# Log-sum-exp over rows of 1024: where the closing barrier waits for the last store, and which engine checks the last sums' upper range

## The chip, the cores and the metric

One core of one Trainium2 chip. The metric is the device time of one execution in microseconds (us); a kernel is quoted by the median of its runs.

## The reference

```
x: float32 [32, 512, 1024]                  # 16384 rows of 1024
max_x = max(x, axis=-1)
out   = max_x + log(sum(exp(x - max_x)))    # float32 [32, 512]
```

## The kernel before

The 67 MB of input are loaded once, in 16 loads of shrinking size, into a ring on chip. ScalarE takes exponentials without subtracting the maximum; VectorE, or ScalarE's own accumulator for a few rows, adds them up; ScalarE takes the logarithm. Dropping the maximum is safe only if each sum lies in a range, so the kernel checks the sums at the end. Every bad sum adds at least 1e17 to `count` by a matmul, and `count` below 1e15 means "all fine". If not, a branch leads to a slow, safe program. The data never take it.

```python
def check(c0, c1, i):                       # called for sums 0..118, and last for 119..126
    first = nc.vector.tensor_scalar(out=clamped[:, c0:c1], in0=sumexp[:, c0:c1],
        scalar1=LOW, scalar2=HIGH, op0=ALU.max, op1=ALU.min)
    counted = nc.vector.scalar_tensor_tensor(out=clamped[:, c0:c1], in0=clamped[:, c0:c1],
        scalar=0.0, in1=sumexp[:, c0:c1], op0=ALU.bypass, op1=ALU.not_equal,
        accum_out=bad[:, i : i + 1])
    nc.tensor.matmul(count, lhsT=bad[:, i : i + 1], rhs=far, start=i == 0, stop=False)
# ... loads, exponentials, sums (cut) ...
nc.scalar.activation(out=res[:, W:NC], in_=sumexp[:, W:NC], func=AF.Ln)          # L208
nc.sync.dma_start(out=out_rows, in_=res[:, 0:W])                                 # L209
last_store = nc.sync.dma_start(out=out_rest, in_=res[:, W:NC]).ins               # L210
# ... check of the last row, check(LATE, LAST, 1), two more matmuls into count (cut) ...
nc.vector.tensor_scalar(out=fine, in0=count, scalar1=HIGH, scalar2=None, op0=ALU.is_lt)
all_fine = nc.values_load(fine[0:1, 0:1], engines=ENGINES, ...)                  # ScalarE, VectorE
with tc.If(all_fine < 1, ...):                                                   # the safe program (cut)
```

The program closes with a barrier that the framework writes. Each engine reports by a drain that adds 1 to a "gather" semaphore; GpSimdE's **collecting** instruction waits for 4 reports, its **releasing** instruction lets the others go on, then GpSimdE **clears** the kernel's semaphores, and a second barrier of the same kind ends the program. In front of its report, SyncE waits for everything that is open. The kernel before arranges that the store is the last item of that list:

```python
def look_at_store_last(program):
    # ... find SyncE's drain with the long list of waits (cut) ...
    waits = sorted(drain.sync_info.on_wait, key=lambda wait: wait.id != store)
```

Of the kernel before, what the change touches and what calls it, by code (L numbers as in the profile page):

```python
# [9 lines left out]
LOW, HIGH = 1e-15, 1e15  # L10
# [4 lines left out]
def kernel(  # L15
# [5 lines left out]
    nc = tc.nc  # L21
# [5 lines left out]
    ALU = mybir.AluOpType  # L27
# [4 lines left out]
    NC = n // P  # L32
# [29 lines left out]
    LATE = 119  # L62
    LAST = NC - 1
# [6 lines left out]
    sumexp = stats.tile([P, NC], fp32, name="sumexp")  # L70
    res = stats.tile([P, NC], fp32, name="res")
    clamped = stats.tile([P, NC], fp32, name="clamped")
    bad = stats.tile([P, 4], fp32, name="bad")
    fine = stats.tile([1, 1], i32, name="fine")
    far = stats.tile([P, 1], fp32, name="far")
    ones = stats.tile([P, 1], fp32, name="ones")
    last_exp = psum.tile([P, d], fp32, name="last_exp")
    count = psum.tile([1, 1], fp32, name="count")
# [5 lines left out]
    def source(e0, size):  # L84

        assert e0 >= W * d or e0 + size <= W * d
        return x_rest[:, e0 - W * d : e0 - W * d + size] if e0 >= W * d else x_rows[:, e0 : e0 + size]

    def without_wait(ins, group, reason):

        tc.declare_no_dep(ins.ins, group=group, reason=reason)

    def in_this_order(first, then):

        info = mybir.DependencyInfo(mybir.DependencyClass.NoSync, mybir.DependencyReason.DATA)
        tc.add_manual_dep(then.ins, first.ins.name, info, reason="order on one engine")


    def check(c0, c1, i):
        first = nc.vector.tensor_scalar(  # L100
            out=clamped[:, c0:c1], in0=sumexp[:, c0:c1],
            scalar1=LOW, scalar2=HIGH, op0=ALU.max, op1=ALU.min,
        )
        counted = nc.vector.scalar_tensor_tensor(  # L104
            out=clamped[:, c0:c1], in0=clamped[:, c0:c1], scalar=0.0, in1=sumexp[:, c0:c1],
            op0=ALU.bypass, op1=ALU.not_equal, accum_out=bad[:, i : i + 1],
        )
        nc.tensor.matmul(count, lhsT=bad[:, i : i + 1], rhs=far, start=i == 0, stop=False)  # L108
        return first, counted

    ln = counted = None
    c = 0
# [3 lines left out]
    for i, (size, ops) in enumerate(loads):  # L116
        if here + size > RING * d:
            assert here == p
            p = here = 0
        dma = nc.sync.dma_start(out=ring[:, here : here + size], in_=source(done, size)).ins  # L120
        if i == 0:
            first_load = dma
        end = here + size
        done += size
        for k, (how, s) in enumerate(ops):
            rows = ring[:, p : p + s * d].rearrange("p (c d) -> p c d", d=d)
            sums = sumexp[:, c : c + s]
            if how == "A":
                assert here == p
                v = ring[:, p : p + d]  # L130
                o = v if c < LAST else last_exp
                exp = nc.scalar.activation(out=o, in_=v, func=AF.Exp, accum_out=sums)  # L132
                here += d
            else:
                upto = end if k + 1 == len(ops) else p + s * d
                v = ring[:, here:upto]
                exp = nc.scalar.activation(out=v, in_=v, func=AF.Exp)  # L137
                here = upto
            assert p + s * d <= here <= end
            without_wait(exp, "loads", "the slot's earlier users came before this load")  # L140
            without_wait(exp, "exps", "the slot's earlier users came before this load")
            without_wait(exp, "sums", "the slot's earlier users came before this load")
            tc.add_to_no_dep_group("exps", exp.ins)
            if ln:
                in_this_order(ln, exp)
                ln = None
            added = []
            if how == "R":
                added = [nc.vector.reduce_sum(out=sums, in_=rows, axis=AX.X)]  # L149
            elif how == "T":  # L150
                for r in range(s):
                    lo = rows[:, r, 0:H]
                    added.append(
                        nc.vector.scalar_tensor_tensor(  # L154
                            out=lo, in0=lo, scalar=1.0, in1=rows[:, r, H:d],
                            op0=ALU.mult, op1=ALU.add, accum_out=sums[:, r : r + 1],
                        )
                    )
            for add in added:
                tc.declare_no_dep(add.ins, dma, reason="ScalarE has waited for it")  # L160
                without_wait(add, "loads", "they came before this one")
            for add in added:
                tc.add_to_no_dep_group("sums", add.ins)
                if counted:
                    in_this_order(counted, add)
                    counted = None
            c += s
            p += s * d
            last_row = v
        assert here == end  # L170
        tc.add_to_no_dep_group("loads", dma)
        if c == LATE:
            ln = nc.scalar.activation(out=res[:, 0:W], in_=sumexp[:, 0:W], func=AF.Ln)  # L173
            in_this_order(exp, ln)
            _, counted = check(0, LATE, 0)

    def start_early(program):

# [9 lines left out]
        )  # L188
        top.insert(k, first)

    def look_at_store_last(program):


        block, k, drain = next(
            (b, k, i) for b in program.main_func.blocks for k, i in enumerate(b.instructions)
            if i.engine == mybir.EngineType.SP and isinstance(i, mybir.InstDrain)
            and i.sync_info and len(i.sync_info.on_wait) > 2
        )
        store = last_store.sync_info.on_update[0].id
        waits = sorted(drain.sync_info.on_wait, key=lambda wait: wait.id != store)  # L200
        assert waits[0].id == store and len(waits) == len(drain.sync_info.on_wait)
        sync = mybir.SyncInfo(on_wait=waits, on_update=list(drain.sync_info.on_update))
        block.instructions[k] = drain.__replace__(sync_info=sync)

    nc.at_finalize(start_early)
    nc.at_finalize(look_at_store_last)

    nc.scalar.activation(out=res[:, W:NC], in_=sumexp[:, W:NC], func=AF.Ln)  # L208
    nc.sync.dma_start(out=out_rows, in_=res[:, 0:W])  # L209
# [5 lines left out]
    low = nc.vector.tensor_scalar(  # L215
        out=bad[:, 2:3], in0=bad[:, 3:4], scalar1=LOG_LOW, scalar2=None, op0=ALU.is_lt
    )
    first, _ = check(LATE, LAST, 1)
    in_this_order(add, seen)
    in_this_order(low, first)  # L220
    nc.tensor.matmul(count, lhsT=bad[:, 2:3], rhs=far, start=False, stop=False)  # L221
    nc.tensor.matmul(count, lhsT=sumexp[:, LAST:NC], rhs=ones, start=False, stop=True)  # L222
    nc.vector.tensor_scalar(out=fine, in0=count, scalar1=HIGH, scalar2=None, op0=ALU.is_lt)  # L223
    all_fine = nc.values_load(
        fine[0:1, 0:1], engines=ENGINES, min_val=0, max_val=1,
# [2 lines left out]
    with tc.If(all_fine < 1, preferred_fallthrough_block=False):  # L228
        with tc.tile_critical(sync_engine=mybir.EngineType.Activation):
            with nc.semaphore("landed") as landed, nc.semaphore("ready") as ready:  # L230
                rows = 0
                steps = 0
                for c0 in range(0, NC, RING):
# [6 lines left out]
                    for c1, c2 in ((c0, edge), (edge, c0 + s)):  # L240
                        if c1 == c2:
                            continue
                        nc.scalar.dma_start(
                            out=ring[:, (c1 - c0) * d : (c2 - c0) * d],
# [5 lines left out]
                        out=neg, in_=v, op=ALU.max, axis=AX.X, negate=True  # L250
# [3 lines left out]
                        out=v, in0=v, in1=neg[:, :, None].to_broadcast([P, s, d])  # L254
# [5 lines left out]
                        out=sumexp[:, c0 : c0 + s], in_=v, axis=AX.X  # L260
# [40 lines left out]
```

## Time and profile before

| | before |
|---|---|
| time | 163.34 us, median of 3 runs (163.11 to 163.40) |
| span in the profile | 161.6 us |
| DMA engines occupied | 97.1% of the span |
| busy: VectorE, ScalarE, TensorE | 115.0, 117.0, 0.5 us |
| from ScalarE's last update (the last sum) to the end of the span | 2.455 us |

Two things help in reading it. The views count only engine work, so the last 1.9 us of the span look empty; there one reads the instructions of the line on which the framework's closing code is booked (L296 here, another number in each kernel). And the trace records each semaphore update with its time. No view prints these, so where I use them I give the number in plain text. The prediction below shows the lines of the page, the chain and the timeline.

### The profile page before, as it was taken

The page shows a single profiled execution, that of the slowest core. Times are in us where ns is not written, and L with a number is a line of the kernel's source. Part 1 is how long each engine was busy: PE and PEld are TensorE (multiplying, and loading weights), DVE is VectorE, ACT ScalarE, POOL GpSimd, SP SyncE. Part 2 cuts the span into 40 slices and gives each one's busy share as a digit, 9 for nine tenths or more (in the row PEclk, how much of TensorE's full clock was granted, in tenths as well). Part 3 has the DMA queues.
Part 4 walks back from the last instruction along what each step waited for, and adds up shares of the span by engine and source line. Part 5 has one row for each costly group of instructions (what it writes and reads, how often), then busy time and mean ns, then how long its engine had stood idle before and what let it go on. Part 6 is the DMA issues. An engine that isn't in the chain of part 4 may idle for free.

```text
span 161.6 us, 227 instructions
## 1 busy us (share of the span) xinstructions
PE 0.5 (0%) x8; PEld 0.3 (0%) x8; DVE 115.0 (71%) x62; ACT 117.0 (72%) x59; POOL 0.2 (0%) x4
## 2 busy tenths in 40 slices
PE   0000000000000000000000000000000000000000
PEld 0000000000000000000000000000000000000000
DVE  0000000899929999399999999999499947995683
ACT  3000059990799609994299949974999999999994
POOL 0000000000000000000000000000000000000000
DMA  8995996996996997998899999996999899999990
GB/s 260 519 519 260 519 519 276 503 519 276 503 519 292 487 519 308 470 519 357 381 438 438 438 422 406 494 520 292 438 438 479 373 456 408 426 430 421 407 378 7
DMA packets 2594, 67.19 MB, mean 416 GB/s; under 512 B 544, under 2 KB 544, under 8 KB 928
## 3 DMA queue, kind: packets, MB, share of 16 engines
q1 hardware_dynamic: 2592, 67.18, 97.1%
q14 instruction: 2, 0.02, 0.0%
HBM read 67.11 MB, written 0.07 MB: 416 GB/s over the span
## 4 chain that ended last, share of the span: by engine, by line
DMA 59%; ACT 19%; DVE 17%; another core or an unknown queue 3%; issue 1%; SPq 0%; PE 0%
DMA ring<-in_x_dram 59%; ACT ring L137 19%; DVE sumexp L149 15%; DVE ring L154 1%; SPq L120 0%; DVE bad L214 0%; PE count L108 0%; DVE clamped L104 0%; DVE bad L215 0%; DVE fine L223 0%; DVE clamped L100 0%; PE count L222 0%; PE count L221 0%
## 5 line engine op out<-in xcount | busy, mean ns | idle before, releaser
L149 DVE TENSOR_REDUCE sumexp<-ring 128x8 f32<-128x8192 f32 (+6 forms) x17 | 102.9, 6107 | 39.7 <-ACT ring L137 39.7
L137 ACT ACTIVATE ring<-ring 128x8192 f32<-128x8192 f32 (+14 forms) x24 | 98.9, 4175 | 41.5 <-DMA ring<-in_x_dram 41.5
L132 ACT ACTIVATE ring<-ring 128x1024 f32<-128x1024 f32 x15 | 15.6, 1043 | 0.0
L154 DVE SCALAR_TENSOR_TENSOR ring<-ring 128x512 f32<-128x512 f32 x17 | 10.9, 687 | 3.5 <-ACT ring L137 3.5
L132 ACT ACTIVATION_READ_ACCUMULATOR ring<-ring 128x1 f32 x15 | 2.8, 189 | 0.0
L80 ACT ACT_TABLE_LOAD x1 | 1.3, 1283 | 0.8 <-PEq L285 0.8
L154 DVE DVE_READ_ACCUMULATOR ring<-ring 128x1 f32 x17 | 1.4, 83 | 0.0
L132 ACT ACTIVATE last_exp<-ring 128x1024 f32<-128x1024 f32 x1 | 1.0, 1013 | 0.0
L108 PE MATMUL count<-far,bad 128*1 128x1 f32 x4 | 0.4, 164 | 159.1 <-DVE clamped L104 159.1
L81 DVE MEMSET ones<- 128x1 f32 x1 | 0.1, 59 | 0.9 <-PEq L285 0.9
L104 DVE SCALAR_TENSOR_TENSOR clamped<-clamped,sumexp 128x119 f32<-128x119 f32 (+1 forms) x2 | 0.5, 226 | 0.1
L108 PEld LDWEIGHTS count<-far,bad 128*1 128x1 f32 x4 | 0.2, 80 | 159.2 <-DVE clamped L104 159.2
L223 DVE TENSOR_SCALAR fine<-count 1x1 int32<-1x1 f32 x1 | 0.1, 145 | 0.4 <-PE count L222 0.4
L100 DVE TENSOR_SCALAR clamped<-sumexp 128x119 f32<-128x119 f32 (+1 forms) x2 | 0.4, 190 | 0.0
L214 DVE TENSOR_REDUCE bad<-ring 128x1 f32<-128x64 f32 x1 | 0.2, 220 | 0.1
L173 ACT ACTIVATE res<-sumexp 128x112 f32<-128x112 f32 x1 | 0.3, 282 | 0.0
L208 ACT ACTIVATE res<-sumexp 128x16 f32<-128x16 f32 x1 | 0.2, 216 | 0.0
L222 PE MATMUL count<-ones,sumexp 128*1 128x1 f32 x2 | 0.2, 164 | 0.0
L221 PE MATMUL count<-far,bad 128*1 128x1 f32 x2 | 0.2, 163 | 0.0
L132 ACT ACTIVATION_READ_ACCUMULATOR last_exp<-ring 128x1 f32 x1 | 0.2, 187 | 0.0
L215 DVE TENSOR_SCALAR bad<-bad 128x1 f32<-128x1 f32 x1 | 0.2, 154 | 0.0
L104 DVE DVE_READ_ACCUMULATOR clamped<-clamped,sumexp 128x1 f32 x2 | 0.2, 83 | 0.0
(7 smaller groups left out, 0.7 us busy)
## 6 DMA issues: line engine op xcount, KB each, us to landing
ring<-in_x_dram SPq DMA_DIRECT2D x1, 6912.0 KB, 31.7
ring<-in_x_dram SPq DMA_DIRECT2D x1, 6400.0 KB, 26.4
ring<-in_x_dram SPq DMA_DIRECT2D x1, 4608.0 KB, 25.1
ring<-in_x_dram SPq DMA_DIRECT2D x1, 3840.0 KB, 23.4
ring<-in_x_dram SPq DMA_DIRECT2D x1, 2816.0 KB, 25.8
ring<-in_x_dram SPq DMA_DIRECT2D x1, 2048.0 KB, 30.1
ring<-in_x_dram SPq DMA_DIRECT2D x1, 1792.0 KB, 22.5
ring<-in_x_dram SPq DMA_DIRECT2D x1, 1408.0 KB, 25.5
```

The source lines that it names most:

```text
L80: nc.scalar.preload_act_table_set("natural_log_exp_and_others")
L100: first = nc.vector.tensor_scalar(out=clamped[:, c0:c1], in0=sumexp[:, c0:c1], scalar1=LOW, scalar2=HIGH, op0=ALU.max, op1=ALU.min,)
L104: counted = nc.vector.scalar_tensor_tensor(out=clamped[:, c0:c1], in0=clamped[:, c0:c1], scalar=0.0, in1=sumexp[:, c0:c1], op0=ALU.bypass, ...
L108: nc.tensor.matmul(count, lhsT=bad[:, i : i + 1], rhs=far, start=i == 0, stop=False)
L132: exp = nc.scalar.activation(out=o, in_=v, func=AF.Exp, accum_out=sums)
L137: exp = nc.scalar.activation(out=v, in_=v, func=AF.Exp)
L149: added = [nc.vector.reduce_sum(out=sums, in_=rows, axis=AX.X)]
L154: nc.vector.scalar_tensor_tensor(out=lo, in0=lo, scalar=1.0, in1=rows[:, r, H:d], op0=ALU.mult, op1=ALU.add, accum_out=sums[:, r : r + 1],)
L173: ln = nc.scalar.activation(out=res[:, 0:W], in_=sumexp[:, 0:W], func=AF.Ln)
L208: nc.scalar.activation(out=res[:, W:NC], in_=sumexp[:, W:NC], func=AF.Ln)
L214: seen = nc.vector.reduce_max(out=bad[:, 3:4], in_=last_row[:, 0 : d // 16], axis=AX.X)
L215: low = nc.vector.tensor_scalar(out=bad[:, 2:3], in0=bad[:, 3:4], scalar1=LOG_LOW, scalar2=None, op0=ALU.is_lt)
```

## The change

Two parts, both at the very end. **Part 1** takes the wait for the last store out of SyncE's list and puts it on GpSimdE's collecting instruction, which saves the steps from SyncE to the barrier. **Part 2** takes the upper limit out of the late check: TensorE adds the late sums themselves into `count`, so a sum above 1e15 pushes `count` over the limit by itself. One small VectorE operation goes, eight matmuls of one column come. The operands of the last sum's matmul change places too (last line of the diff).

```diff
+    def check_late():
+        for c in range(LATE, LAST):
+            nc.tensor.matmul(count, lhsT=ones, rhs=sumexp[:, c : c + 1], start=False, stop=False)
+        low = nc.vector.scalar_tensor_tensor(
+            out=clamped[:, LATE:LAST], in0=sumexp[:, LATE:LAST], scalar=LOW,
+            in1=sumexp[:, LATE:LAST], op0=ALU.max, op1=ALU.not_equal, accum_out=bad[:, 1:2],
+        )
+        nc.tensor.matmul(count, lhsT=bad[:, 1:2], rhs=far, start=False, stop=False)
 ... (check_early is the old check for sums 0 to 118; cut)
-    def look_at_store_last(program):
+    def wait_for_store_in_barrier(program):
 ... (the same search for SyncE's drain; the store's wait is taken out of its list; cut)
+        k, collect = next(
+            (k, i) for k, i in enumerate(block.instructions)
+            if i.engine == mybir.EngineType.Pool and isinstance(i, mybir.InstEventSemaphore)
+        )
+        sync = mybir.SyncInfo(
+            on_wait=moved + list(collect.sync_info.on_wait),
+            on_update=list(collect.sync_info.on_update),
+        )
+        block.instructions[k] = collect.__replace__(sync_info=sync)
 ...
-    nc.tensor.matmul(count, lhsT=sumexp[:, LAST:NC], rhs=ones, start=False, stop=True)
+    nc.tensor.matmul(count, lhsT=ones, rhs=sumexp[:, LAST:NC], start=False, stop=True)
```

More of the change, by code (lines that the diff above doesn't have):

```diff
@@ L96, in in_this_order, with check_early @@
         tc.add_manual_dep(then.ins, first.ins.name, info, reason="order on one engine")
-    def check(c0, c1, i):
-        first = nc.vector.tensor_scalar(
-            out=clamped[:, c0:c1], in0=sumexp[:, c0:c1],
+    def check_early():
+        nc.vector.tensor_scalar(
+            out=clamped[:, 0:LATE], in0=sumexp[:, 0:LATE],
             scalar1=LOW, scalar2=HIGH, op0=ALU.max, op1=ALU.min,
@@ L104, in check @@
         counted = nc.vector.scalar_tensor_tensor(
-            out=clamped[:, c0:c1], in0=clamped[:, c0:c1], scalar=0.0, in1=sumexp[:, c0:c1],
-            op0=ALU.bypass, op1=ALU.not_equal, accum_out=bad[:, i : i + 1],
-        )
-        nc.tensor.matmul(count, lhsT=bad[:, i : i + 1], rhs=far, start=i == 0, stop=False)
-        return first, counted
+            out=clamped[:, 0:LATE], in0=clamped[:, 0:LATE], scalar=0.0, in1=sumexp[:, 0:LATE],
+            op0=ALU.bypass, op1=ALU.not_equal, accum_out=bad[:, 0:1],
+        )
+        nc.tensor.matmul(count, lhsT=bad[:, 0:1], rhs=far, start=True, stop=False)
+        return counted
+    def check_late():
[6 more added lines that the diff above has]
+        nc.tensor.matmul(count, lhsT=bad[:, 1:2], rhs=far, start=False, stop=False)
+        return low
     ln = counted = None
@@ L174 @@
             in_this_order(exp, ln)
-            _, counted = check(0, LATE, 0)
+            counted = check_early()
     def start_early(program):
@@ L199, in look_at_store_last @@
         store = last_store.sync_info.on_update[0].id
-        waits = sorted(drain.sync_info.on_wait, key=lambda wait: wait.id != store)
-        assert waits[0].id == store and len(waits) == len(drain.sync_info.on_wait)
-        sync = mybir.SyncInfo(on_wait=waits, on_update=list(drain.sync_info.on_update))
-        block.instructions[k] = drain.__replace__(sync_info=sync)
+        waits = list(drain.sync_info.on_wait)
+        moved = [wait for wait in waits if wait.id == store]
+        assert len(moved) == 1
+        sync = mybir.SyncInfo(
+            on_wait=[wait for wait in waits if wait.id != store],
+            on_update=list(drain.sync_info.on_update),
+        )
+        block.instructions[k] = drain.__replace__(sync_info=sync)
+        k, collect = next(
+            (k, i) for k, i in enumerate(block.instructions)
+            if i.engine == mybir.EngineType.Pool and isinstance(i, mybir.InstEventSemaphore)
+        )
+        sync = mybir.SyncInfo(
+            on_wait=moved + list(collect.sync_info.on_wait),
+            on_update=list(collect.sync_info.on_update),
+        )
+        block.instructions[k] = collect.__replace__(sync_info=sync)
     nc.at_finalize(start_early)
-    nc.at_finalize(look_at_store_last)
+    nc.at_finalize(wait_for_store_in_barrier)
     nc.scalar.activation(out=res[:, W:NC], in_=sumexp[:, W:NC], func=AF.Ln)
@@ L217 @@
     )
-    first, _ = check(LATE, LAST, 1)
+    first = check_late()
     in_this_order(add, seen)
```

## The prediction

> **What bounds the kernel now.** I read the page first, then the chain that ended last in order of time, then the timeline of the last 3 us, then the groups of the closing line 296 and the waits of the DMA queue, and last the trace's own records of semaphore updates, which no view prints (times from the span's start; I name each one I use).
>
> The page, for the size of things:
>
> ```profile
> span 161.6 us, 227 instructions
> PE 0.5 (0%) x8; PEld 0.3 (0%) x8; DVE 115.0 (71%) x62; ACT 117.0 (72%) x59; POOL 0.2 (0%) x4
> q1 hardware_dynamic: 2592, 67.18, 97.1%
> DMA 59%; ACT 19%; DVE 17%; another core or an unknown queue 3%; issue 1%; SPq 0%; PE 0%
> ```
>
> The DMA engines are occupied for 97.1% of the span. The input, 67.11 MB, sets about 153.5 us of the 161.6. Nothing in the change touches a load, a ring slot, an exponential or a large sum. TensorE and GpSimdE are practically idle. So all that can move is what follows the last loads:
>
> ```profile
> 125.70 27.82 DMA ring<-in_x_dram
> 153.52 0.02 issue
> 153.55 3.51 ACT ring L137 x2
> ...
> 158.81 0.16 DVE L100 TENSOR_SCALAR clamped<-sumexp 128x8 f32<-128x8 f32 x1
> 158.94 0.19 ACT L132 ACTIVATION_READ_ACCUMULATOR last_exp<-ring 128x1 f32 x1
> 159.01 0.17 DVE L104 SCALAR_TENSOR_TENSOR clamped<-clamped,sumexp 128x8 f32<-128x8 f32 x1
> 159.16 0.22 ACT L208 ACTIVATE res<-sumexp 128x16 f32<-128x16 f32 x1
> 159.32 0.11 PEld L222 LDWEIGHTS count<-ones,sumexp 128*1 128x1 f32 x2
> 159.40 0.34 SPq L210 DMA_DIRECT2D out_dram<-res  x1
> 159.57 0.14 DVE L223 TENSOR_SCALAR fine<-count 1x1 int32<-1x1 f32 x1 [0.38 <-PE count L222]
> ```
>
> (The first three lines are of the chain, the others of the timeline.) Two paths leave the last exponential. The **store path**: logarithm L208, store L210 issued at 159.40. The **branch path**: range check on VectorE, sums on TensorE, comparison L223 at 159.57, then the load of the flag into registers and the branch. The printed chain goes down the branch path, but it ends at the last engine work, 159.71, and the span is 161.6: the missing 1.9 us lie in instructions it does not count:
>
> ```profile
> out_dram<-res SPq DMA_DIRECT2D x1, 8.0 KB, 1.4
> SPq L296 <- DVEq L228: 0.6, 1, 0.6
> L296 SPq EVENT_SEMAPHORE  x8: 17/28/624, 159.8 to 161.5; - x8
> L296 POOLq EVENT_SEMAPHORE  x4: 17/17/17, 160.9 to 161.5; - x4
> L296 SPq DRAIN  x3: 7/7/7, 160.8 to 161.1; - x3
> ```
>
> The store lands 1.4 us after its issue. SyncE walks through its list of waits (the 624 ns one is its wait for VectorE's branch), and GpSimdE's collecting instruction runs at 160.9. In exact records: the last of the store's 16 increments comes at 160.817; SyncE's drain, which waits for it, starts at 160.834; its next drain, which reports to the barrier, at 160.889; the report is in at 160.897; GpSimdE collects at 160.921 and its update shows at 160.946; the span ends at 161.589. VectorE's report had come at 160.805, ScalarE's at 160.680, TensorE's at 159.589. So **the store binds the end**, then two SyncE drains, then the barrier. The branch path is 12 ns short of it by VectorE's report.
>
> **What the Trainium skill says.**
> - "DMA: Bandwidth & Descriptors", section "Anatomy of one DMA", puts most of a DMA's fixed cost of about 2 us on the write receipt, after which the semaphore moves. That is for the GpSimdE path; here 8 KB from SyncE take 1.42 us from issue to last increment. The change leaves it as it is.
> - "Perfetto Trace Analysis", section "Sequencer-only Instruction (DRAIN, etc)": the profiler starts such an instruction when all its semaphores are satisfied, and neither the wait nor the propagation of its update is in its duration. The trace agrees in what matters: a drain of 7 ns costs 55 ns from start to the next one's (160.834 to 160.889), so the duration is no measure of a hop. For an event instruction with two waits it differs, since the 624 ns one contains its second wait.
> - "VectorE: DVE Perf Modes", section "The DRAIN you can't avoid", says that a semaphore after each operation costs nothing extra. The trace agrees: the 128x512 sums of L154 start 613 ns apart where each updates a semaphore (151.255, 151.868) and 612 ns where none does (153.968, 154.580).
>
> **Part 1: the wait for the store moves to GpSimdE.** Removed from the path: SyncE's start after the increment (17 ns), the step to its second drain (55), its report (8) and GpSimdE's start after it (24): 160.817 to 160.921, 104 ns. Put there: GpSimdE's own start after the last increment, taken as the same 24 ns as after a report. An event instruction with two waits lasts 28 ns on SyncE against 17 with one, so 11 ns more. Sum: 104 - 24 - 11 = **69 ns saved**, provided that all four reports are in by 160.82. SyncE's is: in the built program it has one wait instruction less (five and a drain, against six and a drain), and its steps are 61 ns. VectorE's, at 160.805, is just in time even without part 2.
>
> **Part 2: the upper check by TensorE.** One small VectorE operation goes (L100 on 128x8). The remaining one can start where that one did, 158.814; its result followed its start by 186 ns (159.009 to 159.195), so it comes at 159.000. TensorE must now wait for the last sum instead, whose ScalarE update is at 159.134. It starts 42 ns after an update (159.195 to 159.237), so at 159.176, and from the first weight load of L222 to the last update it takes 227 ns (159.317 to 159.544): 159.403, against 159.544. The branch path gains **141 ns**: VectorE reports at about 160.66, SyncE at about 160.61. None of it is on the path that sets the end, which is the store's. It buys distance to it, 12 ns becoming about 150.
> Added are eight matmuls of one column for the late sums. Each runs as two passes, about 26 ns apart in the trace, so 8 x 52 = 0.42 us of TensorE. Each waits for its own sum only; the last of these is ready by 158.4 (VectorE 158.40, ScalarE 158.09), 0.7 us before TensorE is needed. They are hidden. VectorE's seven added updates cost nothing, as above. The early half of the check is unchanged.
>
> **Sum:** 69 ns from part 1, 0 from part 2. 163.34 - 0.07 = **163.27 us**.
>
> **Rivals.**
> 1. The branch path takes the store's place. For it: it is only 12 ns behind in this one execution, and the order of the two may change from one execution to another. Against: part 2 takes 141 ns from it. Where the store had landed sooner before, the gain comes from the branch path and is about as large (up to 0.15 us): 163.2.
> 2. The added matmuls are done one after another at the end, if TensorE's order or its waits hold them back. Then up to 0.42 us come on to the branch path, less 0.14 that it gains and 0.15 of distance: 163.4 to 163.5. Against: the listing of the built program has each matmul waiting on one sum's own count.
> 3. GpSimdE reacts to a DMA's semaphore more slowly than SyncE does. No record shows GpSimdE waiting for a DMA. If it took 100 ns in place of 24, the gain would be nothing: 163.34.
> 4. The whole is drowned in what executions differ by. The three runs before lie 0.29 us apart, four times the gain. This is nearly sure for the timed runs: the sign of the measured difference is little better than a coin's, perhaps 65 to 35 for faster.
>
> **Range and chances.** The median of three runs, each spread by about 0.15 us around its middle, with a shift of 0 to -0.15, gives 163.0 to 163.55 for 8 in 10. 2% is 3.3 us; nothing here is of that size, whichever rival holds: faster 0.01, same 0.98, slower 0.01.
>
> **What would show each step right or wrong.** In the trace of the changed kernel: GpSimdE's first closing event instruction should start, or end, within 25 to 45 ns of the store's last increment, and the span should end 0.70 us after that increment instead of 0.772. SyncE should report some 0.2 us before the store lands, VectorE some 0.15. The timeline should show the eight added matmuls spread over 153 to 158.5 us and L223's successor about 0.14 us earlier relative to the end of the last accumulator read. If that comparison is later, rival 2 holds; if GpSimdE starts over 80 ns after the increment, rival 3; if a report comes after the store, rival 1. The predicted time would be wrong if the loads themselves moved, by a change of over 0.3 us in the time of the last load's landing (153.5), for which I see no cause.

## The result

The changed kernel took 163.29 us (163.23 to 163.30, 6 runs) against 163.33 us before (163.11 to 163.48, 6 runs). The ratio is 0.9998, with a 95% interval of 0.9985 to 1.0011: the same.

The page of the changed kernel, the lines that answer to those of before:

```profile
span 161.5 us, 257 instructions
PE 1.9 (1%) x24; PEld 1.0 (1%) x24; DVE 114.9 (71%) x61; ACT 117.0 (72%) x59; POOL 0.2 (0%) x4
q1 hardware_dynamic: 2592, 67.18, 97.1%
```

TensorE has 16 more matmul records (eight matmuls of two passes), VectorE one operation less, and the loads are as they were. The timeline of the changed kernel's last microseconds (start, length, engine, line, operation):

```profile
158.40 0.24 PE L114 MATMUL count<-sumexp,ones 128*1 128x1 f32 x4 [0.42 <-DVE ring L165]
...
158.76 0.16 DVE L115 SCALAR_TENSOR_TENSOR clamped<-sumexp 128x8 f32<-128x8 f32 x1
158.84 0.08 DVE L115 DVE_READ_ACCUMULATOR clamped<-sumexp 128x1 f32 x1
158.89 0.19 ACT L143 ACTIVATION_READ_ACCUMULATOR last_exp<-ring 128x1 f32 x1
...
159.13 0.09 PEld L246 LDWEIGHTS count<-sumexp,ones 128*1 128x1 f32 x2
...
159.35 0.34 SPq L234 DMA_DIRECT2D out_dram<-res  x1
159.36 0.15 DVE L247 TENSOR_SCALAR fine<-count 1x1 int32<-1x1 f32 x1 [0.44 <-PE count L246]
```

Before, the comparison came 0.17 us after the store's issue (159.57 and 159.40); now the two come together. In the list of instructions that touch `count`, the added matmuls stand with their count, their durations in ns (minimum, median, maximum) and their first and last start:

```profile
L114 PE MATMUL count<-sumexp,ones x16: 163/164/165, 154.1 to 158.5; 128*1 128x1 f32 x16
```

They end before TensorE is needed for the last checks at 158.97. The closing code of the changed kernel, in the same form:

```profile
L320 SPq EVENT_SEMAPHORE  x7: 17/28/448, 159.7 to 161.4; - x7
L320 POOLq EVENT_SEMAPHORE  x4: 17/17/43, 160.8 to 161.4; - x4
...
L320 SPq DRAIN  x3: 7/7/7, 160.5 to 161.0; - x3
...
L320 POOLq EVENT_SEMAPHORE_RANGE_CLEAR  x1: 113/113/113, 161.1 to 161.1; - x1
```

SyncE's longest wait, the one for the branch, fell from 624 to 448 ns. SyncE is at its drains at 160.5, where before it stood at 160.8 because of the store. One GpSimdE instruction now lasts 43 ns, where all lasted 17: it is the collecting one, with two waits.

By the trace's own records the store's last increment is at 160.765. GpSimdE's collecting instruction starts 24 ns later (104 before), its update comes 75 ns after the increment (129 before), and the span ends 0.719 us after it (0.772 before). So **the closing path is 53 ns shorter**. The span is 105 ns shorter, but the other 52 ns are not the change's. The store's increment itself came 52 ns sooner, of which 44 ns were there already at the start of the exponential of 128x2304 behind the last large load (153.547 before, 153.503 after).

### The profile page after: what moved, and what is told of

Same layout as the page of the kernel before. It is cut to its first block, busy times and chain, and to the rows that moved or that the text cites. A ratio compares the mean times of both kernels' runs of the same rounds, so it can differ in the third digit from the quotient of the medians. Undisturbed runs are those within 1.5% of the kernel's fastest.

```text
span 161.5 us, 257 instructions
## 1 busy us (share of the span) xinstructions
PE 1.9 (1%) x24; PEld 1.0 (1%) x24; DVE 114.9 (71%) x61; ACT 117.0 (72%) x59; POOL 0.2 (0%) x4
## 4 chain that ended last, share of the span: by engine, by line
DMA 59%; ACT 19%; DVE 16%; another core or an unknown queue 3%; issue 1%; SPq 0%; PE 0%
DMA ring<-in_x_dram 59%; ACT ring L148 19%; DVE sumexp L160 15%; DVE ring L165 1%; SPq L131 0%; DVE bad L238 0%; PE count L119 0%; DVE bad L239 0%; DVE fine L247 0%; PE count L246 0%; DVE clamped L115 0%; PE count L245 0%
## 5 line engine op out<-in xcount | busy, mean ns | idle before, releaser
L114 PE MATMUL count<-sumexp,ones 128*1 128x1 f32 x16 | 1.4, 164 | 3.9 <-DVE ring L165 3.9
L114 PEld LDWEIGHTS count<-sumexp,ones 128*1 128x1 f32 x16 | 0.6, 81 | 4.6 <-DVE ring L165 4.6
L246 PE MATMUL count<-sumexp,ones 128*1 128x1 f32 x2 | 0.2, 164 | 0.0
```

The lines of the kernel that those rows point to most:

```text
L114: nc.tensor.matmul(count, lhsT=ones, rhs=sumexp[:, c : c + 1], start=False, stop=False)
```

## The experiments

Ten runs, all correct. The table holds the measured numbers, from the records of each profile in us. "Last sum" is ScalarE's last accumulator update, 5.583 to 5.587 us after the start of the exponential of 128x2304 in all twelve profiles. So what differs ahead of it is not the tail's. Each version was profiled once, but for the changed kernel (three times) and e6 (twice); in those the two right-hand columns repeat within 2 ns.

| profile | VectorE's report after the last sum | store's last increment after the last sum | end after that increment | end after the last sum |
|---|---|---|---|---|
| before | 1.671 | 1.683 | 0.772 | 2.455 |
| changed | 1.506 | 1.678 | 0.719 | 2.397 |
| e1, part 1 alone | 1.643 | 1.741 | 0.717 | 2.458 |
| e2, part 2 alone | 1.502 | 1.676 | 0.772 | 2.448 |
| e3, reports first | 1.497 | 1.706 | 0.681 | 2.387 |
| e4, sums at the end | 1.857 | 1.679 | 0.859 | 2.538 |
| e5, wait on the release | 1.494 | 1.690 | 0.613 | 2.303 |
| e6, wait on the clear | 1.500 | 1.680 | 0.527 | 2.207 |
| e7, the same, old check | 1.672 | 1.680 | 0.699 | 2.379 |
| changed, again | 1.503 | 1.679 | 0.718 | 2.397 |
| e8, e6 again | 1.502 | 1.680 | 0.529 | 2.209 |
| changed, third | 1.504 | 1.680 | 0.718 | 2.398 |

**My theory:** part 1 gives the whole gain, some 50 ns, because the store sets the end, and part 2 gives nothing by itself because the branch path ends before the store lands. **The rival:** part 2 is what shortens the end, or without it the branch path takes the store's place.

### Part 1 alone

```diff
 (kernel before, with the changed kernel's function)
-    nc.at_finalize(look_at_store_last)
+    nc.at_finalize(wait_for_store_in_barrier)
```

> Part 1 alone: the kernel before with its old range check, the wait for the store on GpSimdE's collecting instruction. Theory (part 1 gives the whole gain): from the store's last increment to the end of the span 0.72 us, as in the changed kernel, against 0.772 before; from ScalarE's last update (the last sum) to the end 2.40 us against 2.455. VectorE's report lies about where the store's last increment does (1.67 and 1.68 us after that update). Rival (part 2 is needed for the gain, since the branch path is only 12 ns behind): the end is 0.74 us or more after the store, set by VectorE's report. Timed: 0.03% below before, which the rounds can hardly resolve.

The end came 0.717 us after the store: the theory's number. Behind the last sum it came at 2.458, not 2.40, because in this execution the store took 1.477 us from issue to last increment (1.418 before, 1.415 in the changed kernel). With those 62 ns against the changed kernel taken off it would be 2.396. The late store also hid the branch path well: VectorE's report was 98 ns ahead of it, so the close finish that I had feared was not seen here. The closing code of this run, with the 43 ns of the changed kernel's collecting instruction:

```profile
L309 POOLq EVENT_SEMAPHORE  x4: 17/17/43, 161.0 to 161.5; - x4
...
L309 SPq DRAIN  x3: 7/7/7, 160.7 to 161.2; - x3
```

In this execution part 1 alone gives the whole gain, 55 ns behind the store. For a close finish there is only an estimate: with the report last, the update comes 38 ns after the report (e4 below: report 178 ns and update 216 ns behind the store), with the store last 75 ns after the store, so a report would cost something only when it comes more than 37 ns behind the store. In the three profiles with the old check it came 98, 12 and 8 ns ahead (e1, before, e7). Timed, 163.44 us against 163.22, ratio 1.0008 (0.9994 to 1.0021): the same.

### Part 2 alone

```diff
 (changed kernel)
-    nc.at_finalize(wait_for_store_in_barrier)
+    nc.at_finalize(look_at_store_last)
```

> Part 2 alone: new range check, the wait for the store stays on SyncE's drain. Theory (part 2 is off the path): VectorE's report comes 0.17 us before the store's last increment in place of 0.012, and yet the end stays 0.772 us after the store's last increment, 2.455 us after ScalarE's last update. Rival (part 2 shortens the end by itself): the end comes up to 0.15 us sooner after ScalarE's last update, 2.31 us. Timed: same as before.

VectorE's report came 0.174 us before the store and the end stayed at 0.772 us behind the store, as before to the nanosecond. Behind the last sum it is 2.448 against 2.455; those 7 ns are the store's. In the closing code SyncE's drains stand at 160.7 again, just behind the store, and no GpSimdE instruction is longer than 17 ns:

```profile
L307 POOLq EVENT_SEMAPHORE  x4: 17/17/17, 160.8 to 161.4; - x4
...
L307 SPq DRAIN  x3: 7/7/7, 160.7 to 161.0; - x3
```

Part 2 is off the path in this form of the kernel. Timed, 163.26 us against 163.22, ratio 1.0008 (0.9994 to 1.0022): the same.

### The two waits in the other order

The changed kernel's collecting instruction saved 15 ns less than I had put down, and its 43 ns pointed to its two waits.

```diff
-            on_wait=moved + list(collect.sync_info.on_wait),
+            on_wait=list(collect.sync_info.on_wait) + moved,
```

> The changed kernel with the two waits of the collecting instruction in the other order: first the four reports, then the store. In the changed kernel the instruction lasted 43 ns (store first) and its update came 75 ns after the store's last increment. Theory (an instruction's second wait is taken up only after its first, so the first one met last costs a further step): with the store second the update comes about 31 ns after the increment, as SyncE's own second wait ended 23 ns after its semaphore's update; the end is 0.675 us after the store instead of 0.719. Rival (two waits cost the same in either order on GpSimdE): 0.719 us again.

The update came 38 ns after the store's last increment (expected 31), not 75, and the end 0.681 us after it (expected 0.675), not 0.719. That is also less than the 49 ns from SyncE's report to this update before (160.897 to 160.946), where the instruction had one wait. In the closing code of this run the collecting instruction is the longest of the GpSimdE ones:

```profile
L320 POOLq EVENT_SEMAPHORE  x4: 17/17/215, 160.7 to 161.4; - x4
```

It starts 24 ns after the last of the four reports, 0.185 us before the store's last increment, and holds the second wait in its 215 ns. The theory holds here, in e3's one profile, and e4 repeats the 38 ns with the report as the late second wait: a wait that is already met still costs when it stands second, and the one that ends last should stand second. Timed, 163.31 us, ratio 1.0001 (0.9987 to 1.0015): the same.

### The added matmuls where they are not hidden

```diff
-        for c in range(LATE, LAST):
-            nc.tensor.matmul(count, lhsT=ones, rhs=sumexp[:, c : c + 1], start=False, stop=False)
         low = nc.vector.scalar_tensor_tensor( ... )
         nc.tensor.matmul(count, lhsT=bad[:, 1:2], rhs=far, start=False, stop=False)
+        for c in range(LATE, LAST):
+            nc.tensor.matmul(count, lhsT=ones, rhs=sumexp[:, c : c + 1], start=False, stop=False)
```

> The changed kernel with its eight added matmuls placed behind the lower check's matmul, so that they run after the small VectorE work instead of beside the large sums. Theory (the added matmuls are free only because they are hidden; 16 passes of some 26 ns cost 0.36 us when they are not): VectorE's report comes 1.86 us after ScalarE's last update in place of 1.51, which is 0.18 us after the store, and the end 2.54 to 2.58 us after it in place of 2.40: about 0.16 us later than the changed kernel. Rival (the branch path does not matter as long as the store is in flight): the end stays at 2.40.

The timeline of this run:

```profile
158.94 0.54 PE L119 MATMUL count<-sumexp,ones 128*1 128x1 f32 x16
...
159.26 0.34 SPq L234 DMA_DIRECT2D out_dram<-res  x1
...
159.62 0.15 DVE L247 TENSOR_SCALAR fine<-count 1x1 int32<-1x1 f32 x1 [0.78 <-PE count L246]
```

Now the 16 passes stand in a row between the small checks, 25 ns apart (0.40 us in all, of which the first three start before the last sum is there), and the comparison comes 0.36 us after the store's issue. VectorE's report came 1.857 us after the last sum (expected 1.86), 0.178 us behind the store, and the end at 2.538, 0.141 us later than in the changed kernel. The 38 ns between 0.178 and 0.141 are the order of the waits again: the late one now stands second, so the update comes 38 ns after it and not 75. So this is the branch path setting the end, and it shows that rival 2 of the prediction has a real cost, which the changed kernel avoids by its order. Timed, 163.44 us against 163.22, ratio 1.0011 (0.9998 to 1.0025).

### The wait for the store later in the barrier

If the close is a fixed row of steps behind the instruction that waits for the store, the wait should go on the last instruction that allows it. The next one is GpSimdE's releasing instruction. The last is the clear, since it resets the store's own semaphore, which must have been counted up by then. The store is still waited for before the program ends.

```diff
 (e5: the releasing instruction in place of the collecting one)
-            if i.engine == mybir.EngineType.Pool and isinstance(i, mybir.InstEventSemaphore)
+            if i.engine == mybir.EngineType.Pool and isinstance(i, mybir.InstEventSemaphore) and not i.sync_info.on_wait
 (e6: the clear in place of the collecting one; its guards for a missing sync_info are cut)
+            if i.engine == mybir.EngineType.Pool and isinstance(i, mybir.InstISA)
```

> The changed kernel with the wait for the store one instruction later: GpSimdE collects the four reports alone, and its releasing instruction waits for the store. Theory (the end is a fixed chain of steps behind the instruction that waits for the store): that instruction starts 24 ns after the store's last increment, where in the changed kernel it starts 128 ns after it, and 0.591 us lie from its start to the end; so the end is 0.615 us after the store against 0.719. Rival (another report, or the branch, takes the place): more than 0.65.

The end came 0.613 us after the store, 0.106 us sooner than in the changed kernel, as expected (0.615). Timed, 163.18 us against 163.23, ratio 1.0000 (0.9987 to 1.0014). (The changed kernel, run again, is the better control.)

> The changed kernel with the wait for the store as late as it may go: on the instruction by which GpSimdE clears the semaphores, the store's among them. Theory (now the branch path sets the end): VectorE reports 1.506 us after ScalarE's last update, GpSimdE collects 24 ns later, the clear follows 264 ns after that, at 1.79, where the store would allow 1.70; from the clear to the end are 0.404 us: the end 2.20 us after ScalarE's last update against 2.397 in the changed kernel, 0.52 us after the store. Rival (the store still sets it): 0.43 us after the store. Timed: 0.12% below the changed kernel, at the edge of what the rounds resolve.

The end came 2.207 us after the last sum (expected 2.20), 0.190 us sooner than in the changed kernel. The clear did not start 24 ns after the store, but 123 ns: it was held by the chain from VectorE's report. In the closing code of e6 it starts at 160.8, where the changed kernel's started at 161.1:

```profile
L320 POOLq EVENT_SEMAPHORE  x4: 17/17/17, 160.5 to 161.1; - x4
...
L320 POOLq EVENT_SEMAPHORE_RANGE_CLEAR  x1: 113/113/113, 160.8 to 160.8; - x1
```

Of those 0.3 us some 0.14 belong to an earlier start of the whole tail (the last sum at 158.949 against 159.087), and the rest is the gain. The branch path now sets the end, so part 2 should be worth something here.

The same with the old check:

```diff
 (kernel before with e6's wait on the clear; check(LATE, LAST, 1) as before)
```

> As the one with the wait on the clear, but with the old range check. Theory (where the branch path sets the end, part 2 is worth what it takes from that path): VectorE reports 1.65 to 1.67 us after ScalarE's last update, the end is 2.34 to 2.36 us after it, so part 2 is worth 0.15 us here, where it was worth nothing with the wait in the collecting instruction. Rival (part 2 is worth nothing anywhere): 2.20 us, as with the new check.

VectorE's report came 1.672 us after the last sum and the end 2.379, which is 0.172 us later than with the new check. The expected end was missed by 20 ns. From the collecting instruction to the clear it took 279 ns in e6 and e7 where I had taken 264 from the kernel before, so a clear that carries a wait started 15 ns later here even though the wait was met (279 ns in e8 too); the rest is VectorE's report, 2 ns above its expected range, and rounding. Part 2 is thus worth 0.17 us as soon as the store no longer hides it. Timed, e6 took 163.06 us, e7 163.19 us and the kernel before 163.23 us: ratios 0.9992 (0.9980 to 1.0005) and 0.9999 (0.9985 to 1.0013).

### The changed kernel again, and the version that beats both

> The changed kernel once more, beside the three above on the same chip, as their control and to see what repeats. Theory: the collecting instruction starts 24 ns after the store's last increment and the end is 0.719 us after it, within 3 ns; VectorE's report 1.50 us after ScalarE's last update. The store's landing itself may differ by tens of ns (it took 1.413 to 1.477 us from issue in the six profiles so far). Timed: same as before, within 0.1%.

The close repeated within 1 ns (0.718 us after the store, the collecting instruction 24 ns after it). Timed, it took 163.39 us against 163.23, ratio 1.0009 (0.9995 to 1.0022): on the other side of 1 from the first result, which shows how little the timed runs say about 53 ns.

The timing of e6 had left its gain inside the interval, so it ran once more beside the changed kernel:

> The kernel with the wait on the clear a second time, in turn with the changed kernel, since the first timing left its gain within the interval. Theory (0.19 us less behind the last sum, as its first trace showed: 2.207 us against 2.397): the mean time is 0.1 to 0.25 us below the changed kernel's of this call, and 0.2 to 0.3 below the kernel before's; the trace again ends 2.20 us after ScalarE's last update. Rival (the gain in the tail is given back in the time that follows the span): the mean times are equal although the spans are not.

> The changed kernel as the control of the run beside it. Theory: the end 0.719 us after the store's last increment and 2.40 us after ScalarE's last update again; the time within 0.1 us of before's. What differs between its executions is the start of the exponential of 128x2304 (153.41 to 153.61 us in the ten profiles so far), while from there to ScalarE's last update it is 5.58 to 5.59 us in every one.

The wait on the clear took 163.15 us (162.99 to 163.21), the changed kernel 163.32 (163.28 to 163.49), the kernel before 163.39 (163.22 to 164.01). Against before the ratio is 0.998 (0.9963 to 0.9997), now clear of 1, though one run of before at 164.01 us helps it. Sturdier is this: in the two together, all 11 runs with the wait on the clear and the new check lie between 162.95 and 163.24 us, and all 10 of the changed kernel between 163.22 and 163.50. The mean differences within each call are 0.28 and 0.22 us, where the traces give 0.19. **This version beats both kernels**, by about 0.2 us of 163.3, that is by about 0.1%; it falls far short of 2%.

One expectation of the third run was too narrow: the exponential of 128x2304 started at 153.616 and 153.626 us in these two profiles, just above the stated 153.61. The lower bound of 153.41 for the ten profiles so far was misread as well, since e6's stands at 153.366. The spread of the times has its source far ahead of the change. The first piece of the load chain (start, length), in the kernel before:

```profile
0.79 40.42 DMA ring<-in_x_dram
```

in e6, whose profiled run was the fastest of all:

```profile
0.79 40.25 DMA ring<-in_x_dram
```

and in e8, the same kernel once more:

```profile
0.80 40.54 DMA ring<-in_x_dram
```

The difference of 0.3 us between two profiles of one kernel is there after 41 us and stays to the end of the loads (0.26 us at the exponential of 128x2304). Why the first loads differ was not tried.

## Why the prediction was right or wrong

- **The bound and the size: right.** The time predicted was 163.27 us and the measured one 163.29; the loads and the large sums did not change. With executions that lie 0.3 us apart, such closeness of the medians is partly luck. The traces test the steps.
- **"The store binds the end": right.** Part 2 alone left the end 0.772 us behind the store, and part 1 alone moved it to 0.717.
- **Part 1, 69 ns: the mechanism right, one term mis-sized.** GpSimdE did start 24 ns after a DMA's increment, as after a report, so rival 3 falls. The term for the second wait, put at 11 ns after SyncE's event instructions, was 26: the instruction lasted 43 ns and not 28. The update came 54 ns sooner than before and the end 53 ns sooner, 0.719 us behind the store and not the predicted 0.70. The reversed order showed that it is the second wait's own cost.
- **Part 2, 141 ns on the branch path and none on the time: right in kind, 24 ns too small.** VectorE's report moved from 1.671 to 1.506 us behind the last sum, 165 ns. TensorE started 42 ns after ScalarE's update, as taken, but needed 205 ns from there to its last update and not 227. The 227 was read where this matmul stood behind two others in TensorE's queue; in e4, where it again stood behind others, with its operands already changed over, it took 227 once more, so the queue and not the operands made the difference. What remains is 2 ns on the way to VectorE's report. VectorE reported 0.172 us before the store (predicted 0.15) and SyncE 0.216 (predicted 0.2).
- **"The added matmuls are hidden": right.** When they are not (e4), VectorE's report comes 0.35 us later (1.857 against 1.506), of which 0.14 us reach the end; rival 2 had put this at 0.42 less 0.14 and less 0.15, that is 0.13. That it comes so close is luck: the distance of 0.15 already contains the 0.14 gained, so the sum should have been 0.42 less 0.15, that is 0.27. Measured, the passes cost 0.35 and the distance was 0.17, which left 0.18, and the order of the two waits gave back 0.04. VectorE's added updates cost nothing, as predicted: its sums of 128x512 start 612 and 613 ns apart in the changed kernel too (153.919, 154.531, 155.144). They are six more behind the early check, seven in place of one, and not the seven of the prediction.
- **Rival 1, the branch path in the store's place:** not in any profile of this kernel; in part 1 alone the store happened to land late. It was made to happen in e4, e6 and e7.
- **A misreading that did no harm:** 153.5 is the landing of the last large load, not of the last load. Three small ones land after it, the last at 157.953 in the kernel before, 37 ns before the last exponential starts. They did not hold the tail up: the last sum follows the exponential of 128x2304 after the same 5.58 to 5.59 us in all twelve profiles.
- **Rival 4, the gain drowned in the spread: right.** The changed kernel measured 0.02% below before in the first rounds, 0.09% above in the second and 0.06% below in the third. "65 to 35 for faster" was about what could be said.

## What to carry to other kernels

At the end of a program, find which event sets the end, and hang the wait for it on the last instruction that truly needs it: here on the clear of the store's semaphore, not on an early report or on the barrier's collecting instruction. Shortening a path that runs beside the binding one gains nothing until that one is moved; part 2 was worth 0 with the wait in the collecting instruction (in the profiles taken, one of them with a late store) and 0.17 us with the wait on the clear. For gains below the spread of executions, measure intervals in the trace from an event that both kernels share.

## What the Trainium skill lacked or had wrong

- "Perfetto Trace Analysis", section "Sequencer-only Instruction (DRAIN, etc)", has the profiled start at the moment when all semaphores are satisfied. For an event instruction with two waits the runs show otherwise: it starts when the wait listed first is met and contains the second (215 ns on GpSimdE with the reports first, 183 ns in e4 with the store first, 624 ns on SyncE before).
- No page that I read tells what a second wait costs or that its order matters. On GpSimdE the instruction lasts 17 ns with one wait and 43 with two, of which the second was met already; its update comes 75 ns after the increment with the late wait first, 38 ns with it second. On SyncE the lengths are 17 and 28 ns.
- The same section of "Perfetto Trace Analysis" names the hidden parts of a sequencer's step but gives no sizes. Here: 24 ns from a semaphore's last update to the start of GpSimdE's waiting instruction, 55 to 59 ns from one drain of SyncE to the next at the close though each is recorded as 7 ns, and 0.404 us from the start of the clear to the end of the program, the same within 2 ns in all twelve profiles.
- "DMA: Bandwidth & Descriptors", section "Anatomy of one DMA", breaks down the fixed cost of about 2 us for the GpSimdE path only, and for SyncE's path the page has a first-byte latency but no time up to the last increment. The 8 KB store from SyncE took 1.41 to 1.48 us from issue to last increment in these profiles.
